# Which blocks get their weight sums from an accumulating DMA, and plain fp32 products in the last eight

## The chip, the cores and the metric

The kernel runs on one core of a Trainium2 chip. The metric is the device time of one launch in microseconds (us); the time of a kernel is the median of several launches. Engines are named as in the profile: PE (TensorE matmul), PEld (its weight loads), DVE (VectorE), ACT (ScalarE), POOL (GpSimd) and SP (SyncE, which here issues DMAs only).

## The reference, cut to what matters

One decoder layer on 256 tokens of width 2048, all in float32. The change touches the MLP: 2048 to 8192, squared ReLU, back to 2048.

```python
def reference(x, p, ...):                  # S = 256, D = 2048, D_FF = 8192
    ...                                    # attention, convolution, gates: r
    h = rms_norm(r, g_mlp[i])
    r = r + jnp.square(jax.nn.relu(h @ w_up[i])) @ w_down[i]
    h = rms_norm(r, g_ple[i])
    r = r + jax.nn.sigmoid(h @ w_ple_gate[i]) * (p[i] @ w_ple_proj[i])
    return r
```

## The kernel before

**Split products.** Nearly every product is made of three float32r matmuls: each operand is split into a high part (a rounded copy by ACT, the helper `high`, L87) and a low part (the rest, a subtraction by DVE, the helper `low`, L101), and PE adds high x high, high x low and low x high. So each weight that is loaded costs an ACT pass, a DVE pass and three matmuls. All matmuls are recorded at L90. The attention products are the exception: they are plain fp32 matmuls without a split.

**The MLP loop.** The loop `for g in range(NU)` (L951) runs over 72 units. Units 0 to 63 each compute one 128-wide tile of the up projection (`ps_up`, 32 matmuls on the one PSUM bank 7), units 64 to 71 one tile of the down projection (`ps_dn`, of the last quarter of w_down). ACT copies the bank out (`up<-ps_up`, by `evacuated` in `take`) before the next unit can write it.

**Blocks.** Three quarters of the down projection are done meanwhile, in 56 blocks, in Winograd's seven-product form of a 2x2 block product. A block has four weight tiles of 128x512, B11, B22, B12, B21 (`raw_s`, four loads of 256 KB, `load_pair`), and takes the activations of two finished up tiles. Its seven products, P1 to P7, have a PSUM bank each:

- the left sides are parts of the activations (`A11`, ...) or sums S1 to S4 of them, made by `sum_u` (L712) once for every pair of up tiles: four DVE operations of 128x128, then a split of all four at once (`s_0`, `s_1`, 128x512);
- the right sides are the tiles B11, B22, B21 or sums of them: T1 = B11+B12, T3 = B22+B12, T2 = B22+T1, T4 = T2+B21, each split in its turn (`t13_hi`, `t13_lo`, `t24_hi`, `t24_lo`, 128x1024 each).

A block is made by `make` (L734) in one unit, and PE does its products (`products`, L803) in the next, after that unit's 32 `ps_up` matmuls. The last eight blocks (pairs 24 to 31 of side 0) are made in two halves over two units: the first half makes S, B11, B22, T1, T3 and gives P1, P3, P5 and P7, the second B21, T2, T4 and P2, P6, P4. They are the work of units 55 to 71.

**Runs.** A block belongs to side 0 or 1 (half of the output columns). Blocks of one side that follow each other are a run, and accumulate in the same seven banks. The order of the blocks gives runs of 4, 8, 8, 8, 8, 8 and 12 blocks, and the last eight blocks are the end of the last run. At the end of each run but the last, the seven banks are copied out by ACT and added to DRAM by seven POOL DMAs (`store`, L821, `part_P<-part`). In the run of eight, the first four blocks take activation sums that the other side has made, the last four make their own.

**Accumulated sums.** For the blocks in `ADDED`, DVE does not add T1 and T3. SP loads B12 twice into a tile `t13` (two buffers in all, `load_added`), and when B11 and B22 have landed, a POOL DMA adds both onto it (L702, `t<-raw_s`). `ADDED` holds every second block from the fifth on: 26 of 56.

**At the end of the loop** `fetch_part` (L833) reads the stored sums of the runs back in four portions (`part_in`), the functions in `jobs` combine them on DVE, four in each half-block unit, and `turn_part` (L859) transposes the results on PE into the same bank 7 (`ps_part`). ACT must copy that out too (`part_out`), before the next unit's matmuls; the copy stands in the list `filling`, whose entries are issued at the places named `fill()`.

**What sets the order.** From unit 2 on, the order of the instructions on each engine is the order in which this code is written; each engine works its list off in order and waits where an operand or a buffer isn't ready. SP's loads too are issued in the order written. Tiles named `raw` and `raw_s` share four buffers.

Of the kernel before, what the change touches and what calls it, by code (L numbers as in the profile page):

```python
# [19 lines left out]
S = 256  # L20
# [18 lines left out]
def hybrid_block_kernel(ctx: ExitStack, tc: tile.TileContext, ins: dict, out: bass.AP):  # L39
# [18 lines left out]
    def slot(shape, dtype, name):  # L58
        return bp.tile(shape, dtype, tag="slot", name=name)
# [23 lines left out]
    def inorder(ins):  # L83
        return tc.keep_in_program_order(ins) if ordered[0] else ins

    def act(*args, **kw):
        return inorder(nc.scalar.activation(*args, **kw))  # L87

    def mm(*args, **kw):
        return inorder(nc.tensor.matmul(*args, **kw))  # L90
# [4 lines left out]
    def load(*args):  # L95
        dma = nc.sync.dma_start(*args)
        return tc.keep_in_program_order(dma) if ordered[0] or ordered_loads[0] else dma
# [5 lines left out]
    dve = vec_ops()  # L103
# [31 lines left out]
    def high(hi, src):  # L135
        act(hi, src, AF.Copy)

    def low(lo, src, hi):
        dve.tensor_sub(lo, src, hi.bitcast(F32))
# [471 lines left out]
    N_GROUP, GROUP = 6, 4  # L611
    N_BOTH = N_GROUP * GROUP
    hP = {}
    uT, u_raw, wS, sums, wU, evac = {}, {}, {}, {}, {}, {}
    banks["acc"], banks["tr"] = [4, 5, 6], [2, 3]
    prod = {}

    units = [("up", i) for i in range(64)] + [("dn", (3, n)) for n in range(8, 16)]
    NU = len(units)
# [4 lines left out]
    items = []  # L624
# [4 lines left out]
    first_of, last_of, seen, run = set(), set(), set(), []  # L629
# [42 lines left out]
    def half_tiles(name):  # L672
        return tuple(wp.tile([P, HALF], F32R, tag=t, name=f"{name}_{t}") for t in ("hi", "lo"))
# [7 lines left out]
        wU[g].append((hi, lo))  # L681
        return lambda: high(hi, raw), lambda: low(lo, raw, hi)

    ADDED = set(items[4::2])

    def pair_part(a, n, d):
        side, j = a
        n += 16 * (j // 8) + 8 * side
        k = 2 * (j % 8) + d
        return ins["w_down"][n:n + 4, :, k * P:(k + 1) * P].rearrange("n p m -> p n m")  # L690
# [3 lines left out]
    def load_pair(a):  # L694
# [3 lines left out]
        for i, block in enumerate(BLOCKS):  # L698
            if i != 2 or a not in ADDED:
                load(raw[:, i, :].rearrange("p (n m) -> p n m", n=4), pair_part(a, *block))  # L700
        if a in ADDED:
            nc.gpsimd.dma_start(wS[a]["t13"], raw[:, 0:2, :], accum_op=ALU.add)  # L702

    def load_added(a):

        wS[a] = {}
        if a in ADDED:
            t = wS[a]["t13"] = wp.tile([P, 2, CW], F32, tag="t", name="t13", bufs=2)
# [3 lines left out]
    def sum_u(j):  # L712

        a11, a12, a21, a22 = (u_raw[2 * j + k][:, t * P:(t + 1) * P] for t in range(2) for k in range(2))
        s = slot([P, 4, P], F32, "s_raw")
        dve.tensor_sub(s[:, 0, :], a21, a22)
        dve.tensor_sub(s[:, 1, :], s[:, 0, :], a11)
        dve.tensor_sub(s[:, 2, :], a11, a21)
        dve.tensor_add(s[:, 3, :], a12, s[:, 1, :])
        return s  # L720

    def evacuated(ps, name, scale=None):
# [7 lines left out]
    def keep(w, names, hi, lo):  # L730
        for i, name in enumerate(names):
            w[name] = hi[:, i * CW:(i + 1) * CW], lo[:, i * CW:(i + 1) * CW]

    def make(a, xs, evacuate, work):  # L734


        w, j = wS[a], a[1]
        raw = w["raw"]
        flat, halves = "p a f -> p (a f)", "p (a f) -> p a f"
        fresh = None  # L740
        if 0 in xs:
            if j not in sums:
                fresh = sum_u(j)
                sums[j] = tuple(slot([P, 4, P], F32R, f"s_{i}") for i in range(2))
            sh, sl = sums[j]
            for i in range(4):
                w[f"S{i + 1}"] = sh[:, i, :], sl[:, i, :]
            hi, lo = half_tiles("b")
            keep(w, ("B11", "B22"), hi, lo)
            src = raw[:, 0:2, :].rearrange(flat)  # L750
            high(hi, src)
            evacuate()
            if fresh is not None:
                high(sh, fresh)
            low(lo, src, hi)
            if a in ADDED:
                t13 = w["t13"]
            else:
                t13 = raw[:, 0:3:2, :]
                dve.tensor_add(t13, raw[:, 0:2, :], raw[:, 2:3, :].to_broadcast([P, 2, CW]))  # L760
            w["raw13"] = t13
        if 2 in xs:
            b21 = w["B21"] = tuple(slot([P, CW], F32R, f"b21_{n}") for n in range(2))
            high(b21[0], raw[:, 3, :])
            evacuate()
            fill()
            dve.tensor_add(raw[:, 1, :], raw[:, 1, :], w["raw13"][:, 0, :])
            if 0 in xs:
                low(b21[1], raw[:, 3, :], b21[0])
                dve.tensor_add(raw[:, 3, :], raw[:, 1, :], raw[:, 3, :])  # L770
                raw24 = raw[:, 1:4:2, :]
            else:
                dve.tensor_add(raw[:, 2, :], raw[:, 1, :], raw[:, 3, :])
                low(b21[1], raw[:, 3, :], b21[0])
                raw24 = raw[:, 1:3, :]
                work()
        if 0 in xs:
            if fresh is not None:
                low(sl, fresh, sh)
            if 2 not in xs:  # L780
                work()
            t13 = half_tiles("t13")
            keep(w, ("T1", "T3"), *t13)
            view = [t.rearrange(halves, a=2) for t in t13]
            high(view[0], w["raw13"])
            fill()
            low(view[1], w["raw13"], view[0])
        if 2 in xs:
            t24 = half_tiles("t24")
            keep(w, ("T2", "T4"), *t24)  # L790
            view = [t.rearrange(halves, a=2) for t in t24]
            high(view[0], raw24)
            fill()
            low(view[1], raw24, view[0])
# [8 lines left out]
    def products(a, x):  # L803
        j = a[1]
        for name, left, b, n0, n1 in PRODUCTS[x]:
            if a in first_of and n0 == 0:
                prod[name] = pp.tile([P, CW], F32, tag=f"b{int(name[1]) - 1}", name=name)
            if left[0] == "A":
                at = slice((int(left[1]) - 1) * P, int(left[1]) * P)
                k = 2 * j + int(left[2]) - 1  # L810
                xs = [uT[k][:, h, at] if k in uT else first_half(k)[:, h, :] for h in range(2)]
            else:
                xs = wS[a][left]
            for n in range(n0, n1):
                mm(prod[name], xs[n == 2], wS[a][b][n == 1], start=a in first_of and n == 0, stop=(a in last_of or a == items[-1]) and n == 2)

# [14 lines left out]
    jobs, turns_due = [], []  # L831
# [27 lines left out]
    def turn_part(u, src):  # L859
        ps = bank("ps_part").rearrange("p (i s) -> p i s", i=2)  # L860
        for i in range(2):
            for t in range(NT):
                inorder(nc.tensor.transpose(ps[:, i, t * P:(t + 1) * P], src[t][:, i * P:(i + 1) * P], ident))

        def out():
            st = slot([P, 2, S], F32, "part_out")
            act(st, ps, AF.Copy)
            nc.gpsimd.dma_start(r_kept[u], st, accum_op=ALU.add)

        filling.append(out)  # L870

    filling = []

    def fill(n=1):
        for _ in range(min(n, len(filling))):
            filling.pop(0)()
# [3 lines left out]
    def first_half(k):  # L880
        return firsts[k // 4][:, k % 4 // 2]
# [56 lines left out]
        r[u] = slot([P, 2, S], F32, f"r_{u}")  # L938
        nc.gpsimd.dma_start(r[u], r_kept[u])

    fetching = {NU - 18: (1, 0), NU - 16: (1, 1), NU - 14: (0, 0), NU - 12: (0, 1)}

    for g in range(2):
        load_raw(g)
# [6 lines left out]
    for g in range(NU):  # L951
        kind, i = units[g]
# [21 lines left out]
        xs = hT if kind == "up" else {k: uT[16 * i[0] + k] for k in range(16)}  # L974
# [19 lines left out]
        halves = []  # L994
# [17 lines left out]
        queue = [] if ending else list(staged[g - 1])  # L1012

        def take():
            if taken:
                return
            taken.append(evacuated(ps, kind))
            if ending:
                side = staged[g - 1][0][0][0]
                filling.extend(lambda name=name: store(side, name) for name in NAMES)  # L1020
            if due and queue:
                products(*queue.pop(0))
                turn_part(*due.pop(0))

        due = [turns_due.pop(0)] if turns_due else []

        def run_jobs():
            for _ in range(min(4, len(jobs))):
                jobs.pop(0)()

        fill(carried)
        if staged[g]:
            make(staged[g][0][0], [x for _, x in staged[g]], take, run_jobs)
        take()
        if g == NU - 1:
            p1 = [evacuated(prod["P1"], "p1", by) for by in (up0, up1)]
            d, e = (slot([P, CW], F32, n) for n in "de")
            scaled(d, prod["P5"], up0, p1[0], ALU.subtract)
            scaled(e, prod["P3"], up0, d)
# [54 lines left out]
    f, c11, u3, c12, c21, c22 = (slot([P, CW], F32, n) for n in ("f", "c11", "u3", "c12", "c21", "c22"))  # L1094
# [148 lines left out]
```

## Time and profile before

| | |
|---|---|
| median of 3 launches | 1442.47 us (1440.68 to 1443.04) |
| the profiled launch | 1441.09 us |
| its span in the profile | 1439.3 us |
| PE busy | 1417.1 us, 98% |
| DVE busy | 1108.2 us, 77% |
| ACT busy | 885.6 us, 62% |
| mean granted clock of PE | 0.995 |

The span is what the trace covers, 1.8 us less than the launch that it was taken from. The loop over the units begins 631 us into the span. In the profile's names buffer numbers are left out: `P` is any of P1 to P7, `t_hi` is `t13_hi` or `t24_hi`, `s` is `s_0` or `s_1`, `t` is the tile `t13`, and `raw_s` is the four tiles of a block. PE's matmuls are pipelined, so that a row's mean duration is more than the distance from one matmul to the next.

### The profile page before, as it was taken

The numbers are of one execution on the slowest core, as the hardware profiler recorded it, in microseconds if no ns is written. First come the engines' busy times: TensorE is split into PE (matmuls) and PEld (weight loads), VectorE is DVE, ScalarE is ACT, GpSimd is POOL, SyncE is SP. The second block draws the span as 40 slices with busy tenths as digits, with TensorE's granted clock in tenths as the row PEclk, the third lists the DMA queues.
The fourth block names the chain that finished last, engine by engine and source line by source line (L and its number), as shares of the span: only waits on it lengthen the run. The fifth ranks groups of instructions, "written<-read, shape, count | busy, mean of one in ns | idle before, by whom it ended". The sixth has DMA issues, their size and how long they took to land.

```text
span 1439.3 us, 19925 instructions
## 1 busy us (share of the span) xinstructions
PE 1417.1 (98%) x7041; PEld 1197.0 (83%) x7041; DVE 1108.2 (77%) x1688; ACT 885.6 (62%) x1446; POOL 211.4 (15%) x321
## 2 busy tenths in 40 slices
PE   9999999999999999999999999999999999989998
PEld 7888888888888888888888888887887877878888
DVE  7676666766565647757999989898979989978984
ACT  6765545554544544546777868676767867665752
POOL 0043464302020200000000101001010100110000
PEclk9999999999999999999999999999999999999999
DMA  9868787766666675645797978989898899996470
GB/s 279 307 224 250 228 248 238 234 208 208 209 207 204 215 256 205 212 165 172 222 299 237 312 232 240 267 238 274 246 254 248 243 296 264 262 276 208 144 259 23
DMA packets 224052, 335.07 MB, mean 233 GB/s; under 512 B 13904, under 2 KB 148304, under 8 KB 209872
## 3 DMA queue, kind: packets, MB, share of 16 engines
q1 hardware_dynamic: 204000, 287.61, 61.1%
q0 software_dynamic: 19808, 46.16, 14.2%
q8 instruction: 55, 0.90, 0.2%
q14 instruction: 45, 0.37, 0.1%
q10 hardware_dynamic: 144, 0.04, 0.0%
HBM read 294.95 MB, written 24.64 MB: 222 GB/s over the span
## 4 chain that ended last, share of the span: by engine, by line
PE 81%; DVE 8%; DMA 6%; issue 3%; ACT 2%; SPq 0%; DVEq 0%; POOLq 0%; ACTq 0%
PE ps_up L90 16%; PE ps_g L90 12%; PE P L90 11%; PE ps_o L90 7%; PE ps_pg L90 6%; PE ps_y L90 6%; DMA raw_s<-in_w_down_dram 4%; PE ps_q L90 3%; PE ps_k L90 3%; PE ps_cx L90 3%; PE ps_cb L90 3%; PE ps_cc L90 3%; PE ps_v L90 3%; PE ps_dn L90 3%; DMA t<-raw_s 2%
## 5 line engine op out<-in xcount | busy, mean ns | idle before, releaser
L101 DVE TENSOR_TENSOR w_lo<-raw,w_hi 128x512 fp32r<-128x512 f32 (+1 forms) x524 | 468.2, 927 | 186.6 <-ACT w_hi L87 161.0
L87 ACT ACTIVATE w_hi<-raw 128x512 fp32r<-128x512 f32 (+1 forms) x524 | 406.9, 816 | 259.3 <-PE ps_g L90 63.3
L90 PE MATMUL ps_up<-x,w_hi 128*128 128x512 f32 x1024 | 255.8, 393 | 6.5 <-ACT part_out L87 3.5
L90 PEld LDWEIGHTS ps_up<-x,w_hi 128*128 128x128 f32 x1024 | 192.4, 189 | 47.6 <-ACT up L87 5.9
L90 PE MATMUL ps_g<-w_hi,x 128*128 128x512 f32 x512 | 158.2, 389 | 0.0
L87 ACT ACTIVATE t_hi<-raw_s 128x1024 fp32r<-128x1024 f32 x86 | 91.2, 1061 | 84.7 <-DVE raw_s L101 84.7
L90 PEld LDWEIGHTS ps_up<-x,w_lo 128*128 128x128 f32 x1024 | 131.3, 191 | 5.0
L90 PE MATMUL ps_up<-x,w_lo 128*128 128x256 f32 x1024 | 132.8, 283 | 0.0
L90 PE MATMUL P<-t_hi,s 128*128 128x512 f32 x336 | 123.4, 394 | 0.3 <-ACT t_hi L87 0.3
L101 DVE TENSOR_TENSOR t_lo<-raw_s,t_hi 128x1024 fp32r<-128x1024 f32 x86 | 103.9, 1221 | 15.5 <-ACT t_hi L87 15.5
L90 PEld LDWEIGHTS ps_g<-w_hi,x 128*128 128x128 f32 x512 | 96.1, 188 | 19.9
L90 PE MATMUL ps_g<-w_lo,x 128*128 128x512 f32 x256 | 99.6, 389 | 0.0
L101 DVE TENSOR_TENSOR raw_s<-raw_s 128x512 f32<-128x512 f32 (+1 forms) x116 | 96.2, 829 | 3.8
L702 POOL DMA_DIRECT2D t<-raw_s x26 | 22.2, 853 | 447.7 <-DMA raw_s<-in_w_down_dram 199.5
L90 PE MATMUL ps_y<-w_hi,x 128*128 128x512 f32 x256 | 79.4, 389 | 0.0
L90 PEld LDWEIGHTS P<-t_hi,s 128*128 128x128 f32 x336 | 63.6, 189 | 13.2 <-ACT t_hi L87 0.7
L101 DVE TENSOR_TENSOR b_lo<-raw_s,b_hi 128x1024 fp32r<-128x1024 f32 x56 | 68.3, 1219 | 3.4 <-ACT b_hi L87 3.4
L90 PE MATMUL P<-t_lo,s 128*128 128x512 f32 x168 | 66.1, 394 | 3.7 <-DVE t_lo L101 3.7
L90 PE MATMUL ps_pg<-x,w_hi 128*128 128x512 f32 (+1 forms) x272 | 69.1, 385 | 0.5 <-DVE x L101 0.5
L87 ACT ACTIVATE up<-ps_up 128x512 f32<-128x512 f32 x64 | 37.6, 588 | 37.2 <-PE ps_up L90 37.2
L87 ACT ACTIVATE a<-a 128x256 f32<-128x256 f32 x128 | 53.2, 415 | 11.6 <-DVE a L101 9.6
L87 ACT ACTIVATE b_hi<-raw_s 128x1024 fp32r<-128x1024 f32 x56 | 58.8, 1050 | 1.8 <-PE ps_dn L90 1.8
(238 smaller groups left out, 2583.2 us busy)
## 6 DMA issues: line engine op xcount, KB each, us to landing
raw<-in_w_up_dram SPq DMA_DIRECT2D x64, 1024.0 KB, 7.6
raw<-in_w_in_dram SPq DMA_DIRECT2D x56, 1024.0 KB, 5.4
raw_s<-in_w_down_dram SPq DMA_DIRECT2D x198, 256.0 KB, 4.4
raw<-in_w_branch_dram SPq DMA_DIRECT2D x16, 1024.0 KB, 5.7
raw<-in_w_o_dram SPq DMA_DIRECT2D x16, 1024.0 KB, 4.9
t<-in_w_down_dram SPq DMA_DIRECT2D x52, 256.0 KB, 5.3
t<-raw_s POOLq DMA_DIRECT2D x26, 512.0 KB, 7.9
raw_first<-in_w_qkv_dram SPq DMA_DIRECT2D x48, 256.0 KB, 6.6
```

Of the source, the lines that this page charges most:

```text
L87: return inorder(nc.scalar.activation(*args, **kw))
L90: return inorder(nc.tensor.matmul(*args, **kw))
L101: return lambda *args, **kw: inorder(getattr(nc.vector, name)(*args, **kw))
L702: nc.gpsimd.dma_start(wS[a]["t13"], raw[:, 0:2, :], accum_op=ALU.add)
```

## The change

There are four edits.

1. `ADDED` is another set. In the middle runs of eight, the first, fifth and seventh block are in it (before: also the third), and in the run's end all of the last eight blocks (before: four of them). It holds 24 blocks (before 26): six third blocks leave, four of the last eight come in.
2. The last eight blocks are `NATIVE`: S1, S3, T1 and T3 are not split, and P5 and P7 are one plain fp32 matmul each instead of three float32r matmuls. The order of the S in their tile changes, so that S2 and S4, which are still split, stand side by side (128x256).
3. The copy of the transposed part, `part_out`, no longer stands in `filling`. It is issued by `out_turned()` at fixed places in the same unit: behind the evacuation in a block's second half, behind the jobs in its first half.
4. The four fetches are made in units 53, 56, 59 and 62 (before 54, 56, 58, 60), and three jobs are done in a unit (before four).

```diff
-    ADDED = set(items[4::2])
+    LAST = len(items) - 8
+    NATIVE = set(items[LAST:])
+    ADDED = {items[n] for n in range(GROUP, LAST) if (n - GROUP) % (2 * GROUP) in (0, 4, 6)} | set(items[LAST:])
...
-            for i in range(4):
-                w[f"S{i + 1}"] = sh[:, i, :], sl[:, i, :]
+            for i, name in enumerate(("S1", "S3", "S2", "S4")):
+                w[name] = sh[:, i, :], sl[:, i, :]
+            if a in NATIVE:
+                w["S1"], w["S3"] = fresh[:, 0, :], fresh[:, 1, :]
+                fresh, sh, sl = (t[:, 2:, :] for t in (fresh, sh, sl))
...
             evacuate()
+            out_turned()
             fill()
...
             if 2 not in xs:
                 work()
-            t13 = half_tiles("t13")
-            keep(w, ("T1", "T3"), *t13)
-            view = [t.rearrange(halves, a=2) for t in t13]
-            high(view[0], w["raw13"])
-            fill()
-            low(view[1], w["raw13"], view[0])
+            out_turned()
+            if a in NATIVE:
+                w["T1"], w["T3"] = w["raw13"][:, 0, :], w["raw13"][:, 1, :]
+                fill()
+            else:
+                t13 = half_tiles("t13")
+                ...
...
+            if a in NATIVE and b in ("T1", "T3"):
+                if n0 == 0:
+                    mm(prod[name], xs, wS[a][b], start=a in first_of, stop=a in last_of or a == items[-1])
+                continue
...
-        filling.append(out)
+        turned_out.append(out)
...
-    fetching = {NU - 18: (1, 0), NU - 16: (1, 1), NU - 14: (0, 0), NU - 12: (0, 1)}
+    fetching = {53: (1, 0), 56: (1, 1), 59: (0, 0), 62: (0, 1)}
...
-            for _ in range(min(4, len(jobs))):
+            for _ in range(min(3, len(jobs))):
```

PE in unit 56, behind the matmuls of `ps_up`: the products of the first half of the first of the last eight blocks. Before:

```order
L90 MATMUL P3_10788<-b_hi_11076,s_1_11075 128x512
L90 MATMUL P5_10792<-t13_hi_11089,s_0_11074 128x512
L90 MATMUL P5_10792<-t13_lo_11090,s_0_11074 128x512
L90 MATMUL P5_10792<-t13_hi_11089,s_1_11075 128x512
L90 MATMUL P7_10796<-t13_hi_11089,s_0_11074 128x512
L90 MATMUL P7_10796<-t13_lo_11090,s_0_11074 128x512
L90 MATMUL ps_up_57_11212<-x_4789,w_hi_11167 128x512
```

and now:

```order
L90 MATMUL P3_10775<-b_lo_11068,s_0_11065 128x512
L90 MATMUL P3_10775<-b_hi_11067,s_1_11066 128x512
L90 MATMUL P5_10779<-t13_10806,s_raw_11060 128x512
L90 MATMUL P7_10783<-t13_10806,s_raw_11060 128x512
L90 MATMUL ps_up_57_11194<-x_4789,w_hi_11153 128x512
```

Five matmuls here, and P7's third one in the next unit, have become two, which read the accumulated tile `t13` itself.

ACT in unit 57, where the second of the last eight blocks is begun and, before, the first part was transposed. Before:

```order
L87 ACTIVATE b_hi_11267<-raw_s_11116 128x1024
L87 ACTIVATE up_11270<-ps_up_57_11212 128x512
L87 ACTIVATE s_0_11265<-s_raw_11260 128x512
L87 ACTIVATE part_in_11127<-part_in_11127,scales_5620 128x256 x2
L87 ACTIVATE t13_hi_11290<-raw_s_11116 128x1024
L87 ACTIVATE part_out_11293<-ps_part_11276 128x512
```

and now unit 59, the first of its kind with a transposed part:

```order
L87 ACTIVATE b_hi_11427<-raw_s_11271 128x1024
L87 ACTIVATE up_11430<-ps_up_59_11372 128x512
L87 ACTIVATE s_0_11425<-s_raw_11420 128x256
L87 ACTIVATE part_out_11446<-ps_part_11435 128x512
L87 ACTIVATE w_hi_11497<-raw_11356 128x1024
```

`part_out` stood behind `t13_hi`, which waits for DVE's sum in `raw_s`; now nothing that waits for the block's weight sums stands ahead of it.

SP's loads around the `t13` tile of the fourth of the last eight blocks (with the semaphores that each row waits for in brackets; `raw_11455` is the up weight of unit 62, `part_in` are the seven reads of a fetch):

```order
L96 DMA raw_11356<-in_w_up_dram 128x2048 [waits DMAHW1_49,DMAHW0_49,DVE_49]
L96 DMA t13_11358<-in_w_down_dram 128x4x128 [waits DMASW1_49,DVE_49,PE_49]
L96 DMA t13_11358<-in_w_down_dram 128x4x128 [waits DMAHW2_49]
L96 DMA part_in_11361<-part_0_P2_5547 128x256 [waits DMAHW3_49]
L96 DMA part_in_11361<-part_0_P4_5549 128x256 [waits DMAHW4_49]
L96 DMA part_in_11364<-part_0_P3_5544 128x256 [waits DMAHW5_49]
L96 DMA part_in_11364<-part_0_P5_5545 128x256 [waits DMAHW6_49]
L96 DMA part_in_11367<-part_0_P1_5543 128x256 [waits DMAHW7_49]
L96 DMA part_in_11369<-part_0_P7_5546 128x256 [waits DMAHW0_49]
L96 DMA part_in_11369<-part_0_P6_5548 128x256 [waits DMAHW1_49]
L96 DMA raw_11455<-in_w_up_dram 128x2048 [waits DMAHW2_49,DVE_49]
L96 DMA raw_s_11457<-in_w_down_dram 128x4x128 [waits DMAHW3_49,DVE_49]
```

The load into a `t13` buffer now waits for PE too, that is for product P7 of the block two before, and the up weight of a later unit stands behind it in SP's list.

More of the change, by code (lines that the diff above doesn't have):

```diff
@@ L716, in sum_u @@
         dve.tensor_sub(s[:, 0, :], a21, a22)
-        dve.tensor_sub(s[:, 1, :], s[:, 0, :], a11)
-        dve.tensor_sub(s[:, 2, :], a11, a21)
-        dve.tensor_add(s[:, 3, :], a12, s[:, 1, :])
+        dve.tensor_sub(s[:, 2, :], s[:, 0, :], a11)
+        dve.tensor_sub(s[:, 1, :], a11, a21)
+        dve.tensor_add(s[:, 3, :], a12, s[:, 2, :])
         return s
@@ L781, in make @@
                 work()
-            t13 = half_tiles("t13")
-            keep(w, ("T1", "T3"), *t13)
-            view = [t.rearrange(halves, a=2) for t in t13]
-            high(view[0], w["raw13"])
-            fill()
-            low(view[1], w["raw13"], view[0])
+            out_turned()
[4 more added lines that the diff above has]
+                t13 = half_tiles("t13")
+                keep(w, ("T1", "T3"), *t13)
+                view = [t.rearrange(halves, a=2) for t in t13]
+                high(view[0], w["raw13"])
+                fill()
+                low(view[1], w["raw13"], view[0])
         if 2 in xs:
@@ L868, in out, with out_turned @@
             nc.gpsimd.dma_start(r_kept[u], st, accum_op=ALU.add)
-        filling.append(out)
-    filling = []
+        turned_out.append(out)
+    filling, turned_out = [], []
+    def out_turned():
+        while turned_out:
+            turned_out.pop(0)()
     def fill(n=1):
@@ L1023, in take @@
                 turn_part(*due.pop(0))
-        due = [turns_due.pop(0)] if turns_due else []
+        due = [turns_due.pop(0)] if turns_due and queue else []
         def run_jobs():
-            for _ in range(min(4, len(jobs))):
+            for _ in range(min(3, len(jobs))):
                 jobs.pop(0)()
@@ L1034, in hybrid_block_kernel @@
         take()
+        out_turned()
         if g == NU - 1:
```

## The prediction

> **What bounds the kernel now.** I first cut the loop into stretches by the starts of its `ps_up` and `ps_dn` groups and read the windows view: units 24 to 55, units 56 to 70, units 39 to 46 alone, and two short windows inside unit 57.
>
> ```profile
> core 0: us, PE busy (x) PEld busy (x) DVE busy (x) ACT busy (x) POOL busy (x), PEclk, DMA share, GB/s
> 846.90:1184.15 337.25, 330.25 (x1676) 280.00 (x1675) 299.93 (x401) 242.26 (x357) 37.03 (x44) 0.99 0.90 253
> 1184.15:1319.07 134.92, 127.50 (x671) 108.10 (x670) 119.04 (x184) 89.34 (x130) 17.26 (x23) 0.97 0.90 264
> 1000.79:1087.97 87.18, 85.24 (x425) 71.97 (x426) 78.08 (x105) 62.76 (x92) 9.40 (x11) 0.98 0.90 253
> 1200.60:1203.50 2.90, 0.23 (x2) 0.00 (x0) 2.87 (x6) 2.07 (x4) 0.00 (x0) 0.91 1.08 323
> 1203.50:1206.00 2.50, 2.46 (x6) 1.99 (x7) 2.50 (x4) 2.47 (x4) 0.66 (x2) 0.50 0.83 254
> ```
>
> PE is near full in both long stretches, but the last window shows it "busy" at half clock, so I measure by the distance between groups instead. The chain of waits (start, us, what) gives the pace without a stall:
>
> ```profile
> 1021.74 5.55 PE ps_up L90 x32
> 1027.29 4.78 PE P L90 x21
> 1032.07 5.55 PE ps_up L90 x32
> ...
> 1303.34 5.55 PE ps_dn L90 x32
> 1308.89 2.29 PE P L90 x10
> 1311.18 5.55 PE ps_dn L90 x32
> 1316.72 2.51 PE P L90 x11
> ```
>
> A full unit takes 5.55 + 4.78 = 10.33 us, and a product matmul 4.78 / 21 = 0.2276 us. The two units of a halved block take 5.55 + 2.51 = 8.06 and 5.55 + 2.29 = 7.84 us. Units 24 to 55 are 30 full units and one halved block: 30 x 10.33 + 8.06 + 7.84 = 325.8 us, against 337.25 measured. **11.5 us** are lost there. Units 56 to 70 are eight of 8.06 and seven of 7.84, with eight transposes between them (0.44 us for four matmuls of `ps_part`, row below): 64.5 + 54.9 + 3.5 = 122.9 us, against 134.92. **12.0 us** are lost there.
>
> Where they are lost, by the chain (of the whole span, then of the last run), the waits (us in total, times, longest) and the timeline (start, us, engine, what, [wait and what ended it]):
>
> ```profile
> 1145.03 12.41 DMA raw_s<-in_w_down_dram
> 1158.01 2.52 DMA t<-raw_s
> 1160.53 5.46 issue
> ```
>
> ```profile
> 1201.94 1.06 ACT t_hi L87
> 1203.00 0.49 ACT part_out L87
> 1203.54 7.19 PE ps_up L90 x32
> ...
> 1212.11 0.44 PE ps_part L863 x4
> ```
>
> ```profile
> ACT t_hi L87 <- DMA t<-raw_s: 23.5, 4, 6.7
> ```
>
> ```profile
> PEld ps_up L90 <- ACT part_out L87: 4.4, 2, 3.1
> PEld ps_dn L90 <- ACT part_out L87: 3.2, 2, 2.8
> ```
>
> ```profile
> 1159.31 1.22 DVE L101 TENSOR_TENSOR b_lo<-raw_s,b_hi 128x1024 fp32r<-128x1024 f32 x1
> ...
> 1165.93 1.06 ACT L87 ACTIVATE t_hi<-t 128x1024 fp32r<-128x1024 f32 x1 [5.70 <-DMA t<-raw_s]
> 1169.20 0.50 PE L90 MATMUL P<-t_lo,s 128*128 128x512 f32 x1 [1.36 <-DVE t_lo L101]
> 1173.69 0.50 PE L90 MATMUL ps_up<-x,w_hi 128*128 128x512 f32 x1 [1.02 <-ACT up L87]
> ```
>
> The wait of `t_hi` for the accumulating DMA occurs four times in units 24 to 55: at the third blocks, whose products stand in units 30, 38, 46 and 54. The block's tiles take 12.41 us to land, the accumulation begins at 1158.01 only and lets ACT go at 1165.93; then `t_lo` is late on PE, and the bank's copy `up` behind it. So the full stretch is PE-bound but for four late third blocks. In units 56 to 70 the order on ACT is the limit in four places: `part_out` behind a late `t_hi`, and PE behind `part_out`, up to 3.1 us, followed by the half clock of the 2.50 us window.
>
> **The change part by part.** *Edit 1 in the middle runs.* The accumulation of six third blocks goes; DVE makes their two sums and splits them as before.
>
> ```profile
> L101 DVE TENSOR_TENSOR raw_s<-raw_s 128x1024 f32<-128x1024 f32 x30 | 36.8, 1225 | 1.0
> L101 DVE TENSOR_TENSOR t_lo<-t,t_hi 128x1024 fp32r<-128x1024 f32 x26 | 31.7, 1218 | 0.3 <-ACT t_hi L87 0.3
> L87 ACT ACTIVATE t_hi<-t 128x1024 fp32r<-128x1024 f32 x26 | 27.4, 1052 | 23.5 <-DMA t<-raw_s 23.5
> L101 DVE TENSOR_TENSOR s<-s_raw,s 128x512 fp32r<-128x512 f32 x32 | 21.9, 685 | 2.1 <-ACT s L87 2.0
> ```
>
> DVE gets one operation of 1.225 us per run. In units 39 to 46 it was busy 78.08 us; with 1.2 more that is 79.3, against 8 x 10.33 = 82.6 at PE's pace, so it is hidden, though with only 3.3 us of cover: without that it would cost 1.2 per run, 5 over the four. For block 54's sums: its tiles have landed by 1157.4 (1145.03 + 12.41); a DVE sum begun behind `b_lo`, at 1160.5 (1159.31 + 1.22), gives `t_hi` and `t_lo` by 1164.0 (+ 1.225 + 1.05 + 1.22), and PE asks for them at 1167.4 (unit 54 begins at 1160.53, + 5.55 + six products at 0.2276). So the wait goes, and nothing late replaces it. Bounds: nothing gained (the loads themselves are the limit) to 11.5. I take 11.5 less 0.8 for run switches that still cost a little: **-10.7**. Fewer transfers (256 KB and 512 KB per third block) only help.
>
> *Edits 2 and 3, and edit 1 in the last run.* Removed are, per halved block, a `t_hi` on ACT (1.05), a `t_lo` on DVE (1.22), half of the split of S (about 0.27 of 0.685), and in four blocks DVE's sum (1.225). DVE has 119.04 - 8 x 1.22 - 8 x 0.27 - 4 x 1.225 = 102.2 us left, far under PE; ACT has 89.34 - 8.4. `part_out` no longer stands behind a `t_hi`. PE is what is left. It loses 16 times three float32r matmuls, 0.683 us, and gains 16 plain fp32 ones, each of 512 columns. No such matmul stands in the trace at that width; the nearest are the attention's plain ones:
>
> ```profile
> L90 PE MATMUL ps_s<-qkT 128*128 128x256 f32 x16 | 4.8, 380 | 0.0
> L90 PE MATMUL ps_s<-qkT 128*128 128x128 f32 x16 | 3.0, 272 | 0.0
> ```
>
> ```profile
> 110.93 0.81 PE L90 MATMUL ps_s<-qkT 128*128 128x128 f32 x4
> ```
>
> From 128 to 256 columns a record grows by 108 ns, 0.844 ns per column, so 512 columns take 0.432 us. Each such instruction leaves two records, so it costs 0.864 us: 0.18 more than what it replaces, 16 x 0.18 = **+2.9**. The lower bound is the pace of one float32r matmul per record (2 x 0.2276: 16 x -0.23 = -3.6), the upper is no overlap at all (596 ns by the same growth, twice: 16 x 0.51 = +8.2). I take the middle value, since the four in the timeline row overlap.
>
> So PE's own work in the last run becomes 122.9 + 2.9 = 125.8 us, against 134.92: -9.1. I leave 2.0 for the turns, because bank 7 is still copied out twice per turn, and in a second half only P2 (0.68 us) lies between the end of `ps_up` and the transposes; the copy `up` takes ACT 4.75 / 8 = 0.59 us of that:
>
> ```profile
> 1184.15:1319.07 134.92, 47.31 (x256) 40.53 (x255) 4.75 (x8) 0.97 0.90 264
> ```
>
> That gives **-7.1**. The bounds are -15 (native at its lowest, no wait) to 0 (rival B).
>
> *Transfers.* Each newly accumulated block of the last run loads 256 KB more and accumulates 512 KB:
>
> ```profile
> q1 hardware_dynamic: 204000, 287.61, 61.1%
> q0 software_dynamic: 19808, 46.16, 14.2%
> ...
> raw<-in_w_up_dram SPq DMA_DIRECT2D x64, 1024.0 KB, 7.6
> raw_s<-in_w_down_dram SPq DMA_DIRECT2D x198, 256.0 KB, 4.4
> ...
> t<-raw_s POOLq DMA_DIRECT2D x26, 512.0 KB, 7.9
> ```
>
> Over the span of 1439.3 us, a megabyte took 0.611 x 1439.3 / 287.61 = 3.06 us of all 16 engines on q1 and 0.142 x 1439.3 / 46.16 = 4.43 on q0. A block adds 0.262 x 3.06 + 0.524 x 4.43 = 3.1 us, four add 12.5. The last run had 0.90 x 134.92 = 121.4 and would have 133.9, more than PE's 125.8. Shares over one occur (1.08 in the short window above), because a packet's time includes waiting, so this is no hard limit; I take it as hidden by tiles loaded up to two units ahead, with rival B for the other case.
>
> The Trainium skill, "SBUF — State Buffer", section "A bandwidth-pool intuition that's wrong (but worth ruling out)", gives about 358 GB/s between HBM and one core. The last run moved 264 GB/s over 134.92 us, 35.6 MB; with 3.1 MB more this rule would ask for an estimated 108 us and leave B no room, while the short window's 323 GB/s at share 1.08 says that the engines' own time runs out first. I follow the row.
>
> *The new wait.* SP's `t13` load now waits for P7 of the block two before, and a later unit's up weight and `raw_s` loads stand behind it. P7 ends with a unit's products. A load let go then has the next two units' `ps_up` and one set of products before PE can miss it, 8.06 + 5.55 = 13.6 us, and the loads take 4.4 to 7.6 us to land (rows above). I cost it at nothing.
>
> *Edit 4* spreads 28 reads and the jobs more evenly; each job set is still done before its turn, and I cost it at nothing (a job early or late moves idle DVE time only, since 102 of 126 us are busy).
>
> **Sum.** The profiled launch took 1441.09 (span 1439.3 and 1.8 around it): 1441.09 - 10.7 - 7.1 = 1423.3. The median, 1442.47, lies 1.4 above it, so I say **1424.5** for the median.
>
> **The rivals.**
>
> *B: the last run becomes bound by its transfers.* 133.9 us of engine time do not fit into 125.8 us, and the run takes 133.9: it gains 1.0 only, and the time is 1442.47 - 10.7 - 1.0 = 1431 to 1432. For it: a share of 0.90 before the addition. Against it: 323 GB/s was moved in a window, and 38.7 MB in 125.8 us would be 308.
>
> *C: the third blocks stay late.* If the loads themselves, not the accumulation, decide, or DVE's further 1.2 us stands ahead of something due, the middle runs gain nothing: 1442.47 - 7.1 = 1435.4. For it: 12.41 us for the load and only 3.3 us of cover on DVE. Against it: the 3.4 us between 1164 and 1167.4 above.
>
> *D, slower: SP waits for PE.* The `t13` load holds back the up weight and the next `raw_s` until P7 is through. It decides from the point where those tiles take over 13.6 us to land. At 18 us each of the six later blocks would cost 4.4, 26 in all: 1424.5 + 26 = 1450.5. For it: 12.41 us has been seen for one load of `raw_s`, in a stretch with less demand. Against it: medians of 4.4 and 7.6, and a `t13` load that waits delays no more than one unit.
>
> *E: no change.* B and C together, 1442.47 - 1.0 = 1441.5: the third blocks stay late and the last run is bound by its transfers. Both would have to fail at once, so this is small.
>
> **How the numbers follow.** My forecast has 0.70, B 0.14, C 0.08, D 0.05, E 0.03. The range starts below the forecast where the allowances of 0.8 and 2.0 turn out to be zero and the fp32 matmul somewhat cheaper (1424.5 - 2.8 - 2.2 = 1419.5) and reaches over B to 1434; it leaves out C, D, E and a lucky fp32 price. A difference of 0.2%, 2.9 us, is what a measurement of this kernel can tell from no change. Faster by more than that are the forecast, B and most of C (0.91), slower is D (0.05), no change the rest (0.04).
>
> **What would show it right or wrong.** Right: units 30, 38, 46 and 54 at 10.33 us; no wait of `t_hi` for `t<-raw_s` there, and a `raw_s` sum of 1.2 us of DVE in its place; units 56 to 70 at about 8.6 and 7.6 us (5.55 + 6 x 0.2276 + 2 x 0.864, and 5.55 + 9 x 0.2276) with a turn's 0.44 on top; no wait for `part_out` over 1 us; P5 and P7 with records of about 596 ns at 0.43 distance. B would show as shares over 1.05 with `w_hi` waiting for `raw`, D as SP's loads of `raw` starting late and `w_hi` waiting in units 60 to 70, C as the same four stalls with `t_hi` or `b_hi` waiting for `raw_s`. The forecast is wrong at the fp32 price if P5 and P7 together take far from 1.73 us, and at edit 1 if the third blocks still lag.

## The result, and the profile after

The changed kernel takes 1426.43 us (four launches, 1424.79 to 1427.64), the kernel before 1442.76 us beside it: a ratio of 0.9884, 95% interval 0.9863 to 0.9905, or 16 us less. The forecast was 1424.5 us, from 1419.5 to 1434.

The windows view of the changed kernel for units 24 to 55 and 56 to 70 (us, then busy times, the granted clock, DMA share, GB/s):

```profile
847.47:1173.16 325.69, 325.69 (x1676) 279.64 (x1675) 310.02 (x412) 249.51 (x364) 34.23 (x40) 1.00 0.92 257
1173.16:1304.91 131.75, 129.15 (x656) 103.82 (x655) 100.92 (x167) 76.67 (x119) 20.70 (x27) 0.99 1.00 283
```

Units 24 to 55 took 337.25 us and now take 325.69, which is PE's own pace (325.8 by the prediction). Units 56 to 70 went from 134.92 to 131.75. With 0.6 us more ahead of unit 24 and 0.7 more behind unit 70, that is the difference of the two spans, 13.4 us (from the unrounded times): 11.6 + 3.2 - 0.6 - 0.7. The medians differ by 3 us more, since the profiled launch of the changed kernel, 1427.64, was the slowest of its four, 1.2 above the median, and that of the kernel before, 1441.09, lies 1.7 below the median beside it.

No `t_hi` waits for the accumulating DMA in the middle any more; what is left there is DVE's sum, as this row of the waits says (units 24 to 55):

```profile
ACT t_hi L87 <- DVE raw_s L101: 33.0, 39, 1.5
```

In the last run the chain shows the new products: six float32r matmuls and two plain ones of two records each, then the nine of a second half, then two plain ones alone behind a transpose:

```profile
1178.87 3.10 PE P L90 x10
1181.97 5.60 PE ps_up L90 x32
1187.57 2.06 PE P L90 x9
...
1196.56 0.44 PE ps_part L878 x4
1196.99 1.72 PE P L90 x4
```

A plain product takes (3.10 - 6 x 0.2276) / 2 = 0.867 us, and 0.86 by the last row. Most of what is left of the last run's loss stands in unit 64, the first of the `ps_dn` units, by the timeline:

```profile
1245.82 3.88 ACT L87 ACTIVATE w_hi<-raw 128x1024 fp32r<-128x1024 f32 x4
1250.13 0.57 ACT L87 ACTIVATE dn<-ps_dn 128x512 f32<-128x512 f32 x1
...
1250.76 0.66 PE L878 MATMUL ps_part<-ident,part_in 128*128 128x128 f32 x4 [1.87 <-ACT dn L87]
1251.25 3.29 PE L90 MATMUL P<-t,s_raw 128*128 128x512 f32 x4
```

In this unit the weights of two units are split, as the splitting is two units ahead from here on, so ACT makes four `w_hi`, without a wait ahead of them, before the copy `dn`, and PE waits 1.87 us for the bank. After that wait two plain products take 3.29 us, with 0.62 of the clock granted to PE (windows view, the end of the wait and what follows):

```profile
1248.50:1250.70 2.20, 0.39 (x2) 0.00 (x0) 2.20 (x3) 2.20 (x4) 0.00 (x0) 1.00 0.09 30
1250.70:1254.50 3.80, 3.74 (x9) 1.87 (x10) 3.77 (x7) 3.02 (x6) 1.75 (x2) 0.62 0.99 281
```

A second profile of the same program (run 3 below) has the same wait of 1.87 us in unit 64, and behind it the full clock; the two products take 1.88 us in that view:

```profile
1250.12 0.66 PE L878 MATMUL ps_part<-ident,part_in 128*128 128x128 f32 x4 [1.87 <-ACT dn L87]
1250.62 1.88 PE L90 MATMUL P<-t,s_raw 128*128 128x512 f32 x4
```

```profile
1250.07:1253.87 3.80, 3.75 (x15) 2.53 (x16) 3.77 (x7) 3.02 (x6) 1.75 (x2) 1.00 0.92 242
```

So the low clock followed this wait in one launch and not in the other. Units 64 and 65 take 21.3 us, and 19.6 in the second profile. Before they took 21.3 too, but that is a coincidence: there PE waited 1.5 us for `dn` behind four `w_hi`, and 2.4 us for `part_out` at the end of unit 65, which is gone. The transfers do not hold up this wait: in its window they are at 0.09 of their time, and no `w_hi` of this unit waits for its tile.

### The profile page after: what moved, and what is told of

It reads as the page before. It is cut to its first block, busy times and chain, and to the rows that moved or that the text cites. A ratio compares the mean times of both kernels' runs of the same rounds, so it can differ in the third digit from the quotient of the medians.

```text
span 1425.9 us, 19876 instructions
## 1 busy us (share of the span) xinstructions
PE 1415.0 (99%) x7025; PEld 1192.6 (84%) x7025; DVE 1100.7 (77%) x1682; ACT 878.2 (62%) x1438; POOL 207.6 (15%) x319
## 4 chain that ended last, share of the span: by engine, by line
PE 93%; DMA 2%; issue 2%; ACT 1%; DVE 1%; POOL 1%; SPq 0%; POOLq 0%; DVEq 0%; ACTq 0%
PE ps_up L90 24%; PE P L90 18%; PE ps_g L90 12%; PE ps_o L90 7%; PE ps_pg L90 6%; PE ps_y L90 6%; PE ps_k L90 3%; PE ps_q L90 3%; PE ps_v L90 3%; PE ps_dn L90 3%; PE ps_cb L90 3%; PE ps_cx L90 2%; PE ps_cc L90 2%; PE ps_proj L90 1%; DMA r_kept<-part_out 0%
## 5 line engine op out<-in xcount | busy, mean ns | idle before, releaser
L90 PE MATMUL P<-t_hi,s 128*128 128x512 f32 x304 | 110.9, 390 | 0.0
L101 DVE TENSOR_TENSOR raw_s<-raw_s 128x512 f32<-128x512 f32 (+1 forms) x120 | 100.1, 834 | 4.1
L90 PEld LDWEIGHTS P<-t_hi,s 128*128 128x128 f32 x304 | 57.1, 188 | 11.7
L90 PE MATMUL P<-t_lo,s 128*128 128x512 f32 x152 | 59.1, 389 | 0.0
```

The costliest lines, as they stand in the source:

```text
L101: return lambda *args, **kw: inorder(getattr(nc.vector, name)(*args, **kw))
```

## The experiments

Below, a unit's length is the distance between the starts of two groups of `ps_up` or `ps_dn` in the trace. In the changed kernel this gives 8.24 and 8.05 us for the two units of a halved block, where the chain has 5.55 + 3.10 = 8.65 and 5.60 + 2.06 = 7.66; the sums agree within 0.02 us. Each ratio is to the kernel before on the same chip.

**1. The middle runs alone.** On the kernel before:

```diff
-    ADDED = set(items[4::2])
+    LAST = len(items) - 8
+    ADDED = {items[n] for n in range(GROUP, len(items), 2) if n >= LAST or (n - GROUP) % (2 * GROUP) != 2}
```

> The kernel before, with only the six third blocks taken out of the accumulated set (20 blocks); the last run as before. Theory: all of the gain in the middle comes from this, and the middle stretch (units 24 to 55) ends near 325.7 us instead of 337.25, so about 1442.8 - 11.5 = 1431.3 us; units 56 to 70 stay at about 134.9. Rival: the middle's gain needs the other edits too (less load on the queues before unit 56, the later fetches), then units 46 and 54 stay late by 2 to 4 us and the time is about 1436 to 1438.

1427.17 us (1424.22 to 1428.56), ratio 0.9891 (0.9873 to 0.9910): all of the gain, within what can be told apart. The windows view of units 24 to 55 and 56 to 70:

```profile
848.85:1174.55 325.70, 325.70 (x1677) 279.61 (x1676) 309.63 (x411) 248.01 (x362) 34.19 (x40) 1.00 0.91 255
1174.55:1306.13 131.58, 126.10 (x672) 107.14 (x671) 116.38 (x179) 87.29 (x127) 17.31 (x23) 0.99 0.91 264
```

The middle stretch is as the theory has it, to 0.1 us. But units 56 to 70, whose code is that of the kernel before, fell by 3.3 us too, which neither expectation had: unit 57 from 11.33 to 9.28 us and unit 58 from 9.99 to 8.67. In the kernel before, unit 54's delay was still being paid for there: PE's wait for `part_out` ahead of unit 58 fell from 2.70 to 0.81 us. Run 10, which takes that delay away by other means, has the same 9.28 and 8.65 us in these units. So the last run's loss of 12.0 us held 3.3 that belong to the third blocks, and the other edits together (with the four further accumulations) changed units 56 to 70 by 131.75 - 131.58 = 0.2 us, or by -2.5 with the second profile of the changed program (129.12, run 3). In run 1, PE's weight loads still wait 5.6 us for `part_out` in the last run (7.6 before):

```profile
PEld ps_dn L90 <- ACT part_out L87: 3.1, 2, 2.8
PEld ps_up L90 <- ACT part_out L87: 2.5, 2, 1.2
```

**2. The last run alone.** On the changed kernel, the third blocks are accumulated again:

```diff
-    ADDED = {items[n] for n in range(GROUP, LAST) if (n - GROUP) % (2 * GROUP) in (0, 4, 6)} | set(items[LAST:])
+    ADDED = set(items[GROUP:LAST:2]) | set(items[LAST:])
```

> The changed kernel with the third blocks of the middle runs accumulated again (30 blocks). Theory: the gains add up, so the last run alone is worth 3.2 us by the traces: units 24 to 55 at about 337 us, units 56 to 70 at about 131.8, about 1439 us. Rival: the two parts overlap (a run that starts late meets other transfers), then the last run's part comes out at 0 or at 6 and more: 1442.8 or under 1437.

1447.42 us, ratio 1.0040 (1.0026 to 1.0053): slower than before, which neither theory had. Units 56 to 70 take 130.5 us, but units 24 to 55 346.4, 9.2 more than before, nearly all of it in unit 53 (19.96 us). Its waits and POOL's own timeline:

```profile
ACT x L87 <- DMA part_P<-part: 10.3, 1, 10.3
```

```profile
1147.99 1.73 POOL L840 DMA_DIRECT2D part_P<-part  x2 [0.59 <-ACT part L87]
1159.23 0.88 POOL L704 DMA_DIRECT2D t<-raw_s  x1 [9.51 <-DVE w_lo L101]
1159.77 1.22 POOL L840 DMA_DIRECT2D part_P<-part  x1
```

The last of the seven stores stands on POOL behind the third block's accumulation, which waits for its late tiles. The store's source is a small tile (`part`, `x`, `part_in`, `part_out`, `up` and others take turns in one pool of such tiles), and ACT is given it for its next `x`. So ACT waits until the store has landed, and PE waits for ACT. In the kernel before, the same store goes out just as late, at 1158.55, 8.5 us into unit 53, and no `x` waits for it. Up to this wait the two programs have the same instructions in the same order but for edit 4: the first fetch, which takes four small tiles ahead of this `x`, stands in unit 53 instead of 54. So the 9.2 us come of the late accumulation and the moved fetch together; no run moved the fetch alone. A third block accumulated late costs, by which tile is handed on, from 1 to nearly 10 us.

**3. The same program again.** The `part_out` copy is put into `filling` again:

```diff
-        turned_out.append(out)
+        filling.append(out)
```

> The changed kernel with part_out in the list of deferred copies again, issued at the next place where one is taken. Theory 1: without t_hi ahead of it the place matters little, 1426 +- 1.5 us. Theory 2: the copy goes a unit later at some turns, PE waits for it as before the change (3.1 and 2.8 us at the longest): 1429 to 1433.

1424.16 us (1423.12 to 1425.34), ratio 0.9874 (0.9854 to 0.9895). On every engine the order of the instructions is that of the changed kernel, row for row: without `t_hi` the two places have nothing between them. So edit 3 does nothing beside edit 2, and the run is a second measurement of the changed program. It tells how well that repeats: the medians are 2.3 us apart, and by the traces units 56 to 70 took 131.75 and 129.12 us, all of the difference in units 61 to 65 (47.9 and 45.2); 1.7 of it stands in units 64 and 65, by the clock behind the same wait, as shown above. Less than some 2.5 us of the last run can't be put down to an edit on one launch.

**4. Without the plain products.**

```diff
-    NATIVE = set(items[LAST:])
+    NATIVE = set()
```

> The changed kernel with the last eight blocks split again, so that P5 and P7 are three float32r matmuls each; all eight still accumulated, part_out still moved. Theory 1, PE sets the last run's pace and the plain products only cost there: minus 16 x 0.18 = 2.9 to 3.1 us, units 56 to 70 at 128.7, about 1423.3 us. Theory 2, the split's 1.05 us on ACT and 1.49 us on DVE per block come back onto the path: DVE has 100.9 + 11.9 = 112.8 us in it, and where it stands ahead of an evacuation the unit gets longer: 1428 to 1432 us.

1432.51 us (1430.99 to 1435.13), ratio 0.9933 (0.9915 to 0.9951), 6 to 8 us slower than with them. Yet units 56 to 61 take 1.5 us less than in the changed kernel, as theory 1 has it, and units 64 and 65 2.7 less (1.0 against its second profile); nearly all is lost in unit 62, 17.09 us against 9.18, and unit 67, 10.75 against 8.74. The waits in units 61 to 64, and POOL's timeline:

```profile
ACT part_out L87 <- DMA r_kept<-part_out: 9.9, 1, 9.9
PE ps_up L90 <- ACT part_out L87: 8.2, 1, 8.2
```

```profile
1227.44 0.85 POOL L704 DMA_DIRECT2D t<-raw_s  x1 [15.91 <-DMA part_in<-part_P]
1227.99 1.19 POOL L883 DMA_DIRECT2D r_kept<-part_out  x1
1239.41 0.86 POOL L883 DMA_DIRECT2D r_kept<-part_out  x1 [10.23 <-ACT part_out L87]
```

In unit 62 it is not the work of ACT or DVE, as theory 2 supposed, but the picture of unit 53 again: on POOL the transfer that adds a transposed part onto r in DRAM (`r_kept<-part_out`) stands behind an accumulation that waits for its tiles, and the next `part_out` is given a tile that this addition still reads. Unit 67 does have theory 2's form: ACT's split of S waits 2.5 us for DVE, `part_out` stands behind it, and PE waits 1.6 us for that.

**5. Fewer accumulations in the last run.** Four of the last eight, as before; for the others DVE makes the sums. As the plain product then reads T3 where DVE soon puts T4, its P7 is not the reference's.

```diff
-    ADDED = {items[n] for n in range(GROUP, LAST) if (n - GROUP) % (2 * GROUP) in (0, 4, 6)} | set(items[LAST:])
+    ADDED = {items[n] for n in range(GROUP, LAST) if (n - GROUP) % (2 * GROUP) in (0, 4, 6)} | set(items[LAST::2])
```

> The changed kernel with four of the last eight blocks accumulated, as before the change; the other four sums are made by DVE. Theory 1: DVE has room (100.9 of 131.75 us, and 4.9 more), so the four further accumulations bought nothing: 1426 +- 1.5 us. Theory 2, they cost something, by POOL's queue and 3.1 us of transfers each: 1422 to 1424.5. Theory 3, they are what keeps DVE off the path: 1429 to 1432.

1428.85 us (1427.03 to 1429.54), ratio 0.9907 (0.9889 to 0.9925). Units 56 to 70 take 133.8 us, and once more it is one unit, 62, with 13.87 us (ACT's copy `up` waits 6.5 us for `r_kept<-part_out`), while unit 64 has 10.53. That is 2.1 and 4.7 us more than in the two profiles of the changed program, and nearly all of it is this one wait, whose place depends on which small tile is handed on. What the four further accumulations are worth in themselves can't be told from it.

**6. The double splitting at another unit.** Unit 62 has the least DVE work, so the weights of two units are split there instead of in unit 64:

```diff
-        reach = 1 if FIRST <= g < NU - 8 else 2
+        reach = 1 if FIRST <= g < NU - 10 else 2
```

> The changed kernel with one number changed: the unit in which the weights of two units are split instead of one is unit 62 instead of 64. Theory: units 64 and 65 (11.89 and 9.39 us, against 8.24 + 8.05 and two transposes of 0.44 = 17.2) are late by 4.1 us since ACT makes four w_hi ahead of the copy dn; with two of them it is done 2 us earlier, and units 64 and 65 fall to about 17.5; unit 62 may lose up to 1. About 1423.3 us. Rival: the transfers (share 1.00 in units 56 to 70) are the limit there, and the stall only moves to another unit: 1426 to 1427.

1430.36 us (1427.31 to 1431.28), ratio 0.9913 (0.9891 to 0.9934). PE's wait of 1.87 us for `dn` is gone, so four `w_hi` ahead of it were its cause. But units 64 and 65 still take 19.1 us, against 21.3 and 19.6 in the two profiles of the changed program and 17.5 by the theory, and unit 63 rose from 8.67 to 12.09: PE waits 3.9 us at its end, and unit 64 begins with 0.57 of the clock over 4 us. The stall moved, as the rival has it, though not shown to be by the transfers' share but by the same wait again, now of `x`, by the waits of the last run:

```profile
ACT x L87 <- DMA r_kept<-part_out: 5.3, 1, 5.3
```

PE's timeline at the start of unit 64, and the window behind it:

```profile
1245.86 5.30 PE L90 MATMUL ps_dn<-x,w_hi 128*128 128x512 f32 x15 [3.90 <-ACT up L87]
```

```profile
1245.90:1249.90 4.00, 4.00 (x11) 3.14 (x12) 2.86 (x6) 1.36 (x4) 0.00 (x0) 0.57 0.84 227
```

**7. POOL's order, first try.** The accumulations of the last eight blocks are written at the end of a unit, behind `out_turned()`:

```diff
+            added.append(lambda: nc.gpsimd.dma_start(wS[a]["t13"], raw[:, 0:2, :], accum_op=ALU.add))
...
         out_turned()
+        while added:
+            added.pop(0)()
```

> The changed kernel with the last eight blocks split again, and their accumulating POOL transfers issued at the end of the unit, behind the transfer of part_out instead of ahead of it. Theory (POOL's queue): in the split kernel unit 62 took 17.09 us and unit 67 10.75 because r_kept<-part_out stood behind t<-raw_s in POOL's queue, and part_out's buffer was not free for the next one; with the order turned round both units are near 8.5, units 56 to 70 at about 126 instead of 137.6, and the time about 1421 us. Rival (transfers are the limit, share near 1): the wait stays, as the same bytes have to move, 1428 to 1432. A second rival: the later accumulation lets t_hi wait on ACT, several units 2 to 5 us longer.

> The changed kernel with the two units' weights split in unit 62 and the accumulating transfers issued at the end of the unit. Theory (POOL's queue): unit 63 of the run with 62 (12.09 us) falls to about 8.7, units 64 and 65 stay near 19, units 56 to 70 at about 129, and the time about 1423.5 us. Rival (transfers are the limit): 1427 to 1430 as in that run.

1432.57 and 1427.81 us (ratios 0.9933 and 0.9904). POOL's transfers did not move: its list is not kept in the order of the code, and `t<-raw_s` stands ahead of `r_kept<-part_out` as in runs 4 and 6. On every engine both have the order of instructions of runs 4 and 6. So POOL's order was not tested; they are second measurements of those programs, with unit 62 at 16.57 (17.09 in run 4) and unit 63 at 11.93 us (12.09 in run 6). These waits come back, unlike the difference of the two launches in run 3.

**8. POOL's order, kept.** Now POOL's transfers of the last run (the accumulations, the additions into the kept r, its loads and the results added to it) are held to the order of the code from unit 56 on, in the split kernel, and with the late accumulations in that of run 6:

```diff
+    def pool_dma(*args, **kw):
+        dma = nc.gpsimd.dma_start(*args, **kw)
+        return tc.keep_in_program_order(dma) if pool_ordered[0] else dma
...
-            nc.gpsimd.dma_start(wS[a]["t13"], raw[:, 0:2, :], accum_op=ALU.add)
+            pool_dma(wS[a]["t13"], raw[:, 0:2, :], accum_op=ALU.add)
```

> The split kernel (last eight blocks split, all accumulated) with POOL's transfers of the last run kept in the order of the code: r_kept<-part_out of unit 61 now stands ahead of the fourth of the last eight blocks' t<-raw_s instead of behind it. Theory (POOL's queue): unit 62 falls from 17.09 to about 8.5 and unit 63 to 8.2, unit 67 may stay at 10.8, units 56 to 70 at about 128 instead of 137.6: about 1423 us. Rival (the transfers themselves are the limit in this stretch): unit 62 and the time stay, 1431 to 1433 us.

> The changed kernel with the two units' weights split in unit 62, and on POOL the transfers in the order of the code with t<-raw_s issued at the end of its unit, so that r_kept<-part_out of unit 62 stands ahead of it. Theory (POOL's queue): unit 63, 12.1 and 11.9 us in the two kernels with 62 and the old order, falls to about 8.7, units 56 to 70 to about 129, the time to about 1424 us. Rival (transfers are the limit): unit 63 stays at 12 and the time at 1427 to 1430. Second rival: the accumulation, now 2 to 3 us later, makes P5 wait in units 64 or 66.

The split kernel takes 1426.73 us (1425.71 to 1428.78), ratio 0.9897 (0.9882 to 0.9912), 5.8 us less than in run 4. POOL's timeline in units 61 and 62:

```profile
1222.81 0.85 POOL L77 DMA_DIRECT2D r_kept<-part_out  x1 [11.25 <-ACT part_out L91]
1227.23 0.85 POOL L77 DMA_DIRECT2D t<-raw_s  x1 [3.57 <-DMA part_in<-part_P]
1231.19 0.85 POOL L77 DMA_DIRECT2D r_kept<-part_out  x1 [3.11 <-ACT part_out L91]
```

The addition goes out 5.2 us earlier, and unit 62 falls from 17.09 to 8.67 us. So the theory holds for that unit. But units 56 to 70 take 134.4 us and not 128: units 64, 65 and 68 rose to 12.41, 9.68 and 12.05, and `t_hi` waits 10.2 us for `t<-raw_s` in all. That the fixed order puts other transfers behind each other there is likely, but was not followed transfer by transfer. The other kernel takes 1426.81 us (1425.42 to 1428.14), ratio 0.9893 (0.9876 to 0.9909), against 1427.81 and 1430.36 for its two models; its unit 63 stays at 11.49, against the theory: the addition goes out as soon as it can, at 1232.48, but lands 9.73 us later, and `x` still gets its source tile, as the chain says.

```profile
1232.48 9.73 DMA r_kept<-part_out
...
1242.29 0.04 ACT x L91
```

**9. No tile for `part_out`.** In the split kernel with POOL's list as in run 4, the copy is written over the stored sums that the transposes have just read:

```diff
-            st = slot([P, 2, S], F32, "part_out")
             act(st, ps, AF.Copy)
```

where `st` is now the `part_in` tile of the two sums.

> The split kernel (last eight blocks split, all accumulated, POOL's list as there, with t<-raw_s ahead of r_kept<-part_out) with one thing changed: the copy of a transposed part takes no tile of its own from the pool of small tiles, but is written over the stored sums that the transposes have just read. Theory (a small tile is handed on while the slow r_kept transfer still reads it): ACT's wait for r_kept<-part_out in units 61 to 63 goes, unit 62 falls from 17.09 and 16.57 us to about 8.5 and unit 63 to about 8, units 56 to 70 to about 128, and the time to about 1422 us; then the split is no dearer than the plain products. Rival 1 (POOL's order or the transfers are the limit): unit 62 stays over 15 and the time at 1431 to 1433 us. Rival 2: another tile's reuse waits in its place, the time is 1425 to 1429 us, and a different unit is longer by 3 to 6 us.

1430.90 us (1429.67 to 1432.76), ratio 0.9921 (0.9906 to 0.9935). Unit 62 falls to 8.66 us, as the theory has it. But units 56 to 70 take 137.59 us, to the hundredth what they took in run 4, with units 63 and 64 at 13.43 and 12.94: rival 2, at the price of rival 1. DVE's `b` now is what gets the tile, by DVE's timeline:

```profile
1228.35 0.69 DVE L101 TENSOR_TENSOR raw_s<-raw_s 128x512 f32<-128x512 f32 x1
1238.52 0.69 DVE L101 TENSOR_TENSOR b<-raw_s,b 128x512 fp32r<-128x512 f32 x1 [9.47 <-DMA r_kept<-part_in]
```

In four kernels here another user got the tile (`part_out` in run 4, `up` in run 5, `x` in run 6, `b` here) and waited 5 to 10 us for the addition to land. The wait belongs to the pool of tiles and to the late transfer, not to one user.

**10. Why third blocks were late.** On the kernel before, 28 of the 42 stores are left out (each after a side's first seven), so that the stored sums hold only the first run of each side:

```diff
-        how = {"accum_op": ALU.add} if (side, name) in stored else {}
+        if (side, name) in stored:
+            return
```

> The kernel before without the 28 accumulating stores of the middle runs (part_P<-part, 256 KB each), so that the stored sums hold only the first run of each side. Theory: the third blocks' tiles take 12 us to land, and their accumulation comes late, because these stores move at the same time; without them the tiles land in 5 to 7 us, units 30, 38, 46 and 54 take 10.33 us and the time is about 1430 us. Rival: the tiles are issued too late whatever else moves, since their buffers come free late at a run's end, and the four units keep most of their 1 to 4 us: 1438 to 1442 us.

One launch: 1426.85 us. Units 24 to 55 take 325.69 us, and 30, 38, 46 and 54 are at 10.33. Around unit 53, in which the third block of the last switch is made (its `ps_up` begins at 1142.06), the chain and POOL's timeline show

```profile
1142.06 5.55 PE ps_up L90 x32
1147.60 4.78 PE P L90 x21
1152.38 5.55 PE ps_up L90 x32
1157.93 4.78 PE P L90 x21
```

```profile
1137.13 0.85 POOL L702 DMA_DIRECT2D t<-raw_s  x1 [19.04 <-DVE x L101]
```

The accumulation goes out 4.9 us ahead of that unit; before, it went out at 1158.01, 8.0 us into it. So the stores of a run switch were what made the third blocks late. Before, the block's loads were issued 5.0 us into unit 52 and took 11.4 to 12.6 us to land; without the stores they were issued 0.9 us into it and took 3.2 to 3.8 us. The run takes the whole store transfers away, so it doesn't tell by what they slow the loads. In the changed kernel the loads of that block take as long to land as before (three of the four 12.4 to 12.7 us), but no accumulation stands behind them.

## Why the prediction was right, point by point

- **Edit 1 in the middle** (-10.7): measured -11.6, shown by runs 1 and 10. The allowance of 0.8 for run switches was not needed, and DVE's further 1.2 us per run stayed hidden. Rival C is out.
- **The last run** (-7.1): measured -3.2, and -5.8 in the second profile of run 3. The size was wrong, and so was what it was put down to. The step that failed is to take the whole loss of units 56 to 70 as the wait that "the order on ACT is the limit in four places" describes. The waits were there and the edits removed them: PE's weight loads waited 7.6 us for `part_out` before, 5.6 in run 1, and not at all now. But 3.3 us of the 12.0 were the aftermath of unit 54 and go with edit 1 alone (run 1). Against run 1, the parts that this sum of -7.1 is made of are worth +0.2 us in one profile and -2.5 in the other: they took out 2.1 us in units 56 to 60 (44.0 us in run 1, 41.9 now), while units 61 to 70 take 2.3 us more, or 0.4 less in the second profile. Of the 21.3 us of units 64 and 65 before, the 1.5 us behind four `w_hi` were left in place; they were in the trace, but not read from it.
- **The allowance of 2.0 for the turns** was the term that was too small: with 2.9 us for the plain products PE's own work is 125.8 as forecast, so 5.9 us were left over in the first profile and 3.3 in the second, 4.1 of the 5.9 in units 64 and 65. A small part is in the 125.8 itself: where a transpose stands in a block's second half, the chain gives it 0.65 us instead of 0.44.
- **Edit 2, the plain product**: 0.864 us predicted, 0.867 measured; sixteen cost 16 x (0.867 - 0.683) = 2.9 us on PE as forecast. The records were foreseen at 596 ns and have a mean of 640, the slow ones of unit 64 among them:

```profile
L90 PE MATMUL P<-t,s_raw 128*128 128x512 f32 x32 | 16.4, 640 | 0.0
```

- **Edit 3** is nothing beside edit 2 (run 3). **Edit 4** was costed at nothing, as moving idle DVE time only; it wasn't tried alone, but run 2 points to its fetch also moving which small tile is handed on, there at a price of 9 us together with the late accumulation.
- **Rival B** (transfers) is not shown: the share is 1.00 over the last run, near what it supposed, but the wait in unit 64 falls into a window with 0.09. What holds the slower versions (runs 4 to 6 and 9) is small tiles that a late addition on POOL still reads, a rival that the prediction didn't have: it looked at SP's list and left POOL's out. In the changed kernel itself two copies of ACT wait so, `up` 3.3 and `x` 1.8 us, and PE loses about 1 us by them. Whether these additions land late because of the transfers' load is not shown.
- **Rival D** (SP's new wait for P7): there is no wait of `w_hi` for `raw` among the waits of the changed kernel's last run, and one of 2.0 us in its second profile, in a unit that is no longer for it. Its form did occur, on POOL: run 2 is slower than before by such a queue.
- **The sum** came out within 2 us because the middle gave 0.9 more and the last run 3.9 less (1.3 less in the second profile), and the median of the changed kernel lies 1.2 us under its profiled launch. That it came so near is in part luck: the 3.3 us that edit 1 alone brings in the last run were forecast from the other edits, which brought from nothing to 2.5.

What stays open is whether edits 2 to 4 and the four further accumulations are worth anything. With them 1426.43 and 1424.16 us, without them 1427.17 us: from nothing to 3 us. None of the versions tried is clearly faster than the changed kernel.

## What to carry to other kernels

Look for the block that comes just after a burst of stores: an accumulating transfer there adds its own 8 us to tiles that are late already, while the same sum on a compute engine with 3 us of slack costs nothing. And before a loss in one stretch is put down to that stretch, ask how much of it a delay ahead of it has left behind: the cheapest test is to take the earlier delay away alone. On POOL, whose transfers went out in the order of its list in these runs, one that waits for its operands held up not only the transfers behind it but the tiles that they read, and the engine that was handed such a tile next.

## What the runs showed that was not expected

- The wait for a tile that a transfer still reads moves from user to user at nearly the same price: `part_out` in run 4 and `b` in run 9, with units 56 to 70 at 137.59 us both times.
- The same program, order for order, differed by 2.6 us in units 56 to 70 from one profiled launch to another, while units 24 to 55 agreed to 0.01 us in all the runs without a late third block (325.69 or 325.70).
- A wait of PE of 1.87 us in unit 64 was followed by 3.8 us at 0.62 of the clock in one launch, and by the full clock in another launch of the same program: two plain products took 3.29 and 1.88 us.
